# Down product of a streaming-encoder trunk: lower weight parts by ScalarE and an accumulating transfer, and one more seven-product pair

## The chip, the cores and the metric

The kernel runs on one core of one Trainium2 chip. The metric is device microseconds of one execution of the whole program. The kernel before takes 1934.27 us (median of 3 runs, 1934.19 to 1934.36).

A core has five engines with instruction streams of their own: TensorE (PE in the profile; its weight loads are PEld), VectorE (DVE), ScalarE (ACT), GpSimd (POOL) and SyncE (SP), which here only issues transfers. Each engine works through its instructions in order and waits on semaphores for the others. Transfers between HBM and the on-chip memory SBUF run on 16 DMA engines; matmuls accumulate in PSUM.

## The reference, cut to what matters

Two layers run over 256 tokens of width 2048. Layer 0 has a convolution mixer, layer 1 latent attention; each is followed by an MLP. The change lies in the MLP's second product alone:

```python
def sq_relu_mlp(h, w1, w2):
    return jnp.square(jax.nn.relu(h @ w1)) @ w2     # w1: 2048 x 8192, w2: 8192 x 2048

for layer in range(DEPTH):
    ...                                             # mixer, residual
    h = rms_norm(x, norm_mlp_g[layer])
    x = x + sq_relu_mlp(h, mlp_w1[layer], mlp_w2[layer])
```

All values are float32.

## The kernel before, in words

**Split products.** TensorE multiplies in a rounded 32-bit form (`fp32r`). To keep precision, each operand is split: the upper part `hi` is the value rounded by ScalarE (`AF.Copy` into an `fp32r` tile), the lower part `lo = raw - hi` comes from VectorE. A product is then three matmuls (`mm3`, lines 203 to 205): upper by upper, lower by upper, upper by lower. In the second of them the lower part is the activations', in the third it is the weights'. Only the third one reads the weights' `lo`.

**Weights.** `load` (line 153) brings a tile of 1 MB from HBM into one of three `raw` buffers, by SyncE's queue. `split` (line 181) splits it in two halves, `split_half` each: one ScalarE operation of 128x1024 (line 170) and one VectorE operation of 128x1024 (line 174). The `hi` and the `lo` tiles have six buffers each (`WB = 6`), which go round in the order in which the tiles are asked for: the seventh tile takes the buffer of the first, as soon as TensorE has read that for the last time.

**The MLP.** Each MLP is done in two halves of the 8192 hidden columns. A half is an up product (32 loads of `w1`, lines 655 and 656), which gives 32 blocks of 128 hidden rows, and a down product with those 32 blocks, added onto the residual `xs`. So there are four down products in a run: layer 0 halves 0 and 1, layer 1 halves 0 and 1.

**The down product.** It goes over the output columns in two column pairs of 2 x 512 (`n = 0` and `n = 2`). In each, the 32 hidden blocks are taken as 16 pairs of two blocks, and a pair with its 2 x 512 columns and the 2 x 128 tokens is a 2 x 2 by 2 x 2 block product. Two forms are used:

- A *plain quad* (`Sums.plain`, line 559) does the 8 block products, 24 matmuls of 128x512. Its weights are two row blocks, `j = 0` and `j = 1`, of 128x1024; TensorE does all of `j = 0` before `j = 1`.
- A *mixed quad* (`Sums.mixed`, line 546) does seven block products, 21 matmuls, of combined operands in the manner of Strassen and Winograd. VectorE forms the combined weights in `mixed_weights` (line 490: lines 505, 506 and 507 combine, line 498 makes the lower parts), and the combined activations in `mixed_inputs`. It takes four `hi` and four `lo` tiles where a plain quad takes two of each.

`MIXED` (line 44) lists the pairs done by seven products: eight of the 16 in the first three halves, seven in the last. The loop in `mlp` interleaves them with the plain quads by a rule of its own (`HEAD`, `TAIL`, the variable `upto`). With eight and eight, P for plain and M for mixed, the first column pair is P P M M P M M P M P M M P M P P and the second P M P M P M M P M P M P M M P P. In the last half only the first column pair uses this loop; the second goes through `product_A`, whose plain work comes in loads of four row blocks by 512 columns, with the mixed quads put between them.

**Results.** Some column blocks are added onto `xs` by transfers that GpSimd issues (line 578, `accum_op=ALU.add`), others by VectorE.

**Order.** Within the MLP the program's order on each engine is set by the framework's scheduler from the order in which the code is written; the rows that it gives for the changed places stand below.

Of the kernel before, what the change touches and what calls it, by code (L numbers as in the profile page):

```python
# [11 lines left out]
F32R = mybir.dt.float32r  # L12
BF16 = mybir.dt.bfloat16
I32 = mybir.dt.int32
AF = mybir.ActivationFunctionType
ALU = mybir.AluOpType
AX = mybir.AxisListType

P = 128
# [5 lines left out]
NB = 512  # L25
# [15 lines left out]
PAD_O = 56  # L41
WB = 6
LOOK = WB // 2 - 1
MIXED = {(layer, half): (0, 1, 4, 5, 8, 9, 12) + (13,) * (layer + half < 2) for layer in range(2) for half in range(2)}
N_MIXED = 4
HEAD, TAIL = (2, 1), 2

# [32 lines left out]
def trunk_kernel(  # L80
# [26 lines left out]
    nc = tc.nc  # L107
# [4 lines left out]
    wpool = ctx.enter_context(tc.tile_pool(name="wpool", bufs=2))  # L112
# [27 lines left out]
    def nm(s):  # L140
        uid[0] += 1
        return f"{s}_{uid[0]}"
# [10 lines left out]
    def load(srcs, nj, parts=1):  # L153

        raw = wpool.tile([P, nj, sum(src.shape[-1] for src in srcs)], F32, tag="raw", name=nm("raw"), bufs=3)
        for h in range(parts):
            js = slice(h * nj // parts, (h + 1) * nj // parts)
            at = 0
            for src in srcs:
                nc.sync.dma_start(raw[:, js, at : at + src.shape[-1]], src[:, js, :])  # L160
                at += src.shape[-1]
        return raw
# [14 lines left out]
    def split_half(raw, h, eng):  # L177

        return lower_half(*upper_half(raw, h), eng)

    def split(raw, eng):

        half = raw.shape[1] // 2
        parts = [split_half(raw, h, eng) for h in range(2)]

        def at_j(j):
            hi, lo = parts[j // half]
            return hi[:, j % half, :], lo[:, j % half, :]

        return at_j  # L190

# [3 lines left out]
    def rows(w, k0, nk, c0, n):  # L195

        return w[k0 * P : (k0 + nk) * P, c0 : c0 + n].rearrange(
            "(j p) n -> p j n", p=P
        )
# [331 lines left out]
    class Sums:  # L531
# [24 lines left out]
            for ps, i, (wh, wl) in work:  # L556
                mm3(ps, fh[:, i, :], fl[:, i, :], wh, wl, self.first(ps), end and any(ps is u for u in self.u))

        def plain(self, w, k, hi, lo, k0, end, middle=None):

            at_j = split(load([rows(w, k, 2, self.n * NB, 2 * NB)], 2), nc.vector)
            order = [(j, c, t) for j in range(2) for c in range(2) for t in range(T)]
            if end:
                order.sort(key=lambda r: r[1:])
            for i, (j, c, t) in enumerate(order):
                if middle is not None and 2 * i == len(order):
                    middle()
                wh, wl = (a[:, c * NB : (c + 1) * NB] for a in at_j(j))
                ps = self.e[t][c]
                mm3(ps, hi(k0 + j, t), lo(k0 + j, t), wh, wl, self.first(ps), end and j == 1)  # L570
# [38 lines left out]
    def mlp(layer, ssq, next_gain, finish=None, before=None, beside=None, after_up=None):  # L609

        with ExitStack() as cx:
# [22 lines left out]
            for hf in range(HALVES):  # L634
                last = hf == HALVES - 1
                ms = MIXED[layer, hf]
                mixed = sorted({p // 2 for p in ms})
                plain = [g for g in range(ng) if g not in mixed]
                gs = {}
                for g in range(ng):  # L640
# [4 lines left out]
                    for u in range(KC // 4):  # L645
# [3 lines left out]
                        for j in range(4):  # L649
                            k = 4 * u + j  # L650
# [12 lines left out]
                    if g in mixed or g in plain[len(plain) + len(mixed) - N_MIXED :]:  # L663
                        shape = [P, 2, 7, P] if g in mixed else [P, 4, S]
# [4 lines left out]
                    for b2 in range(2):  # L669
# [11 lines left out]
                        if g in mixed:  # L681
                            v = v.rearrange("p k (t n) -> p (k t) n", t=T)
                            h, l = gh[:, b2, : 2 * T, :], gl[:, b2, : 2 * T, :]
                        else:
                            h, l = (a[:, 2 * b2 : 2 * b2 + 2, :] for a in (gh, gl))
# [3 lines left out]
                w, k_lo = mlp_w2[layer], hf * nkh  # L689
# [9 lines left out]
                hi, lo = at_kt(0), at_kt(1)  # L699
# [8 lines left out]
                for n in range(0, NNB - 2 * split_end, 2):  # L708
                    sums = Sums(n, not last or split_end)
                    ks = [2 * p for p in ps]  # L710
                    at, head = 0, HEAD[n // 2]
                    for i, k in enumerate(ks):
                        upto = (len(ms) * (i - head + 1) + (head > 1) * (len(ks) - head - TAIL)) // (len(ks) - head - TAIL + 1)
                        while at < min(upto, len(ms)):
                            mixed_quad(sums, at)
                            at += 1
                        if i == len(ks) - TAIL + 1:
                            sums.join(room)
                        at_end = i == len(ks) - 1
                        sums.plain(  # L720
                            w, k_lo + k, hi, lo, k, at_end,
                            (lambda: [prepare(due.pop(0), out=room, rest=rest) for _ in range(len(due))]) if at_end else None,
                        )
                    sums.close(room)
                    while rest:
                        rest.pop(0)()
                    if last:
                        due += [n, n + 1]
# [29 lines left out]
    with ExitStack() as cx:  # L758
# [235 lines left out]
        with tc.manual_schedule():  # L994
# [214 lines left out]
            mean, scale = (tr_tile()[:, :S] for _ in range(2))  # L1209
# [58 lines left out]
            for m in range(NP):  # L1268
# [4 lines left out]
                for j in range(2):  # L1273
                    k = 2 * m + j
# [19 lines left out]
                for q in {NP - 3: (0, 1, 4), NP - 2: (5, 2, 3), NP - 1: (6, 7)}.get(m, ()):  # L1294
                    t, i = divmod(q, NNB)
# [74 lines left out]
    with ExitStack() as cx:  # L1370
# [58 lines left out]
        raws, parts = {}, {}  # L1429
# [270 lines left out]
        with tc.manual_schedule():  # L1700
# [23 lines left out]
            for k in range(KC):  # L1724
                u, j = divmod(k, 2)
# [23 lines left out]
            for k in range(KC):  # L1749
                u, j = divmod(k, 4)  # L1750
# [59 lines left out]
            for g in range(NG):  # L1810
                for i in range(HG):
                    h = g * HG + i
# [43 lines left out]
    with ExitStack():  # L1856
# [50 lines left out]
        def before(ssq):  # L1907

            for t in range(T):
# [4 lines left out]
                for n in range(NNB - 1):  # L1914
                    gained(t, n)

        mlp(1, ssq, None, finish, before, after_up=load_gf)


# [24 lines left out]
```

## Time and profile before

| | |
|---|---|
| median of the runs | 1934.27 us |
| profiled execution: span from first to last instruction | 1932.5 us |
| the four down products in that span | 478 to 641, 819 to 979, 1419 to 1582, 1760 to 1924 us |
| TensorE busy | 1921.0 us (99%) |
| VectorE busy | 1592.2 us (82%) |
| ScalarE busy | 1095.6 us (57%) |
| GpSimd busy | 249.0 us (13%) |
| moved from HBM | 363.68 MB |

The profile is of one execution. The median of the runs is 1.8 us above the span of that execution; what lies around the span is not in the profile. In a row that groups instructions, the number after x is the count, then come busy time in us, mean ns of one, and, after the second bar, the engine's idle time before these instructions with what ended it. In a row of the timeline the first number is the start in us from the span's start and the second the length; xN merges neighbours. In a row of transfers the last number is the median time from issue to landing.

### The profile page before, as it was taken

How to read it: one execution, taken by the hardware profiler on the slowest of the kernel's cores; microseconds unless marked ns; L12 is line 12 of the kernel's file. 1: busy time of each engine (PE TensorE's matmuls, PEld its weight loads, DVE VectorE, ACT ScalarE, POOL GpSimd, SP SyncE). 2: the span in 40 equal slices, each digit the busy share in tenths (PEclk: the TensorE clock that was granted, in tenths of full speed). 3: DMA queues.
4: the chain of work that ended last, by engine and by line, in shares of the span. 5: the costliest groups of instructions: out<-in, count | busy, mean ns of one | idle time of the engine just before them, and what ended most of it. 6: DMA issues, size and time to landing. Idle time of an engine off the chain costs nothing.

```text
span 1932.5 us, 28477 instructions
## 1 busy us (share of the span) xinstructions
PE 1921.0 (99%) x10725; PEld 1681.5 (87%) x10725; DVE 1592.2 (82%) x2457; ACT 1095.6 (57%) x1636; POOL 249.0 (13%) x208
## 2 busy tenths in 40 slices
PE   9999999999999999999999999999999999999998
PEld 8999888888888888888898998888888888888887
DVE  7999988877999776799976766877789987678998
ACT  5667755554555545555576655555555554455554
POOL 6999200000010100000001420000000010000000
PEclk9999999999999999999999999999999999999999
DMA  7766456665585866655656545465646776665774
GB/s 230 214 183 189 153 189 206 193 194 177 175 251 194 263 195 187 194 174 196 217 176 175 142 134 192 155 216 186 188 162 225 222 248 212 191 196 175 231 219 150
DMA packets 230427, 375.50 MB, mean 194 GB/s; under 512 B 16392, under 2 KB 107792, under 8 KB 230032
## 3 DMA queue, kind: packets, MB, share of 16 engines
q1 hardware_dynamic: 224640, 363.28, 58.7%
q0 software_dynamic: 4320, 7.87, 2.2%
q10 hardware_dynamic: 1328, 2.52, 0.4%
q8 instruction: 84, 1.38, 0.3%
q14 instruction: 55, 0.45, 0.1%
HBM read 363.68 MB, written 2.10 MB: 189 GB/s over the span
## 4 chain that ended last, share of the span: by engine, by line
PE 97%; DVE 2%; DMA 0%; ACT 0%; issue 0%; ACTq 0%; DVEq 0%
PE acc L655 24%; PE acc L205 15%; PE acc L203 15%; PE acc L204 15%; PE acc L656 13%; PE acc L823 8%; PE acc L1287 2%; DVE sum L910 1%; DMA xs<-in_x 0%; PE acc L1535 0%; PE acc L1566 0%; PE acc L1565 0%; PE acc L1536 0%; PE acc L1564 0%; PE acc L1537 0%; PE tr L267 0%
## 5 line engine op out<-in xcount | busy, mean ns | idle before, releaser
L174 DVE TENSOR_TENSOR lo<-raw,hi 128x1024 fp32r<-128x1024 f32 (+2 forms) x509 | 602.2, 1197 | 232.3 <-ACT hi L170 226.6
L170 ACT ACTIVATE hi<-raw 128x1024 fp32r<-128x1024 f32 (+2 forms) x574 | 583.9, 1036 | 361.1 <-PE acc L655 203.7
L655 PE MATMUL acc<-xt,hi 128*128 128x512 f32 x2048 | 710.6, 390 | 0.0
L656 PE MATMUL acc<-xt,lo 128*128 128x256 f32 x2048 | 577.5, 282 | 0.0
L655 PEld LDWEIGHTS acc<-xt,hi 128*128 128x128 f32 x2048 | 384.3, 188 | 80.7
L656 PEld LDWEIGHTS acc<-xt,lo 128*128 128x128 f32 x2048 | 387.1, 189 | 0.2
L497 ACT ACTIVATE hi<-raw 128x1024 fp32r<-128x1024 f32 x248 | 228.7, 948 | 228.3 <-DVE raw L505 134.0
L498 DVE TENSOR_TENSOR lo<-raw,hi 128x1024 fp32r<-128x1024 f32 x248 | 263.9, 1087 | 27.6 <-ACT hi L497 22.5
L203 PE MATMUL acc<-hi,sh 128*128 128x512 f32 x514 | 200.1, 389 | 0.0
L205 PE MATMUL acc<-lo,sh 128*128 128x512 f32 x514 | 200.1, 389 | 0.0
L203 PE MATMUL acc<-hi,gh 128*128 128x512 f32 (+1 forms) x516 | 200.0, 388 | 0.0
L205 PE MATMUL acc<-lo,gh 128*128 128x512 f32 (+1 forms) x516 | 199.9, 387 | 0.0
L204 PE MATMUL acc<-hi,gl 128*128 128x512 f32 (+1 forms) x516 | 199.9, 387 | 0.0
L823 PE MATMUL acc<-xt,hi 128*128 128x256 f32 x1024 | 180.2, 281 | 0.3 <-ACT b L1106 0.2
L204 PE MATMUL acc<-hi,sl 128*128 128x512 f32 x450 | 175.1, 389 | 0.0
L578 POOL DMA_DIRECT2D xs<-v x30 | 26.5, 994 | 1136.4 <-DVE lo L174 703.2
L910 DVE SCALAR_TENSOR_TENSOR sum<-ub,w_dw,sum 128x256 f32<-128x256 f32 x409 | 164.3, 481 | 3.6 <-ACT sum L880 3.0
L174 POOL TENSOR_TENSOR lo<-raw,hi 128x1024 fp32r<-128x1024 f32 x65 | 155.0, 2410 | 17.3 <-ACT hi L170 17.3
L823 PEld LDWEIGHTS acc<-xt,hi 128*128 128x128 f32 x1024 | 154.8, 188 | 1.1 <-ACT xt L1090 0.6
L823 PE MATMUL acc<-xt,lo 128*128 128x256 f32 x512 | 139.2, 279 | 0.0
L205 PEld LDWEIGHTS acc<-lo,sh 128*128 128x128 f32 x514 | 96.5, 188 | 20.4 <-DVE lo L498 0.3
L204 PEld LDWEIGHTS acc<-hi,gl 128*128 128x128 f32 x516 | 96.9, 188 | 19.9
(314 smaller groups left out, 2531.3 us busy)
## 6 DMA issues: line engine op xcount, KB each, us to landing
raw<-in_mlp_w SPq DMA_DIRECT2D x255, 1024.0 KB, 5.5
raw<-in_conv_w_pw SPq DMA_DIRECT2D x62, 512.0 KB, 5.1
raw<-in_conv_w_pw SPq DMA_DIRECT2D x16, 1024.0 KB, 5.1
raw<-in_mla_w_o SPq DMA_DIRECT2D x16, 1024.0 KB, 5.7
raw<-in_mla_w_kv_up SPq DMA_DIRECT2D x32, 256.0 KB, 3.9
xs<-v POOLq DMA_DIRECT2D x30, 256.0 KB, 7.8
raw<-in_mla_w_in SPq DMA_DIRECT2D x8, 576.0 KB, 3.8
raw<-in_mla_w_in SPq DMA_DIRECT2D x4, 1024.0 KB
```

What stands on the lines that cost most here:

```text
L170: nc.scalar.activation(hi, raw[:, js, :], AF.Copy)
L174: eng.tensor_tensor(lo, raw, hi.bitcast(F32), op=ALU.subtract)
L203: nc.tensor.matmul(ps, sh, mh, start=start, stop=False)
L204: nc.tensor.matmul(ps, sl, mh, start=False, stop=False)
L205: nc.tensor.matmul(ps, sh, ml, start=False, stop=stop)
L497: nc.scalar.activation(hi, src, AF.Copy)
L498: nc.vector.tensor_tensor(lo, src, hi.bitcast(F32), op=ALU.subtract)
L655: nc.tensor.matmul(ps[b], wh[:, bs], xhl(k), start=k == 0, stop=False)
L656: nc.tensor.matmul(ps[b][:, :S], wl[:, bs], xh(k), start=False, stop=k == KC - 1)
L823: nc.tensor.matmul(pss[c][b][:, :S], w[i][:, bs], (xh, xl)[j](k), start=k == i + j == 0, stop=end and k == k0 + nk - 1 and (i, j) == terms ...
L910: nc.vector.scalar_tensor_tensor(out=out, in0=ubs[c][:, w : w + S], scalar=tap(c, w), in1=base, op0=ALU.mult, op1=ALU.add)
L1287: nc.tensor.matmul(ps2[b][t], x_kt(k, t), w[:, bs], start=k == g == i == 0, stop=k == KC - 1 and i == len(group) - 1,)
```

## The change

Two edits.

1. `MIXED` gives the last half (layer 1, half 1) the eighth pair, 13, as in the other three.
2. `Sums.plain` gets a flag `by_sum`, set for the plain quads from number `head` up to the one before the last: five of the first column pair and six of the second. In such a quad the row block `j = 1` is split otherwise: ScalarE writes `lo = -raw`, rounded, and `hi`, and GpSimd issues a transfer that adds the same 512 KB of weights, read from HBM once more, onto `lo`. Row block `j = 0` is split as before. VectorE does one lower part of 128x1024 less in each, ScalarE one operation more. There are 11 such quads in each of the first three halves and five in the last, 38 in all.

```diff
-MIXED = {(layer, half): (0, 1, 4, 5, 8, 9, 12) + (13,) * (layer + half < 2) for layer in range(2) for half in range(2)}
+MIXED = {(layer, half): (0, 1, 4, 5, 8, 9, 12, 13) for layer in range(2) for half in range(2)}
...
+    def split_by_sum(src, raw, eng):
+
+        js = slice(raw.shape[1] // 2, raw.shape[1])
+        shape = [P, raw.shape[1] // 2, raw.shape[2]]
+        hi = wpool.tile(shape, F32R, tag="hi", name=nm("hi"), bufs=WB)
+        lo = wpool.tile(shape, F32R, tag="lo", name=nm("lo"), bufs=WB)
+        nc.scalar.activation(lo, raw[:, js, :], AF.Copy, scale=-1.0)
+        nc.gpsimd.dma_start(lo, src[:, js, :], accum_op=ALU.add)
+        nc.scalar.activation(hi, raw[:, js, :], AF.Copy)
+        parts = [split_half(raw, 0, eng), (hi, lo)]
+
+        def at_j(j):
+            h, l = parts[j // shape[1]]
+            return h[:, j % shape[1], :], l[:, j % shape[1], :]
+
+        return at_j
...
-        def plain(self, w, k, hi, lo, k0, end, middle=None):
+        def plain(self, w, k, hi, lo, k0, end, middle=None, by_sum=False):
 
-            at_j = split(load([rows(w, k, 2, self.n * NB, 2 * NB)], 2), nc.vector)
+            src = rows(w, k, 2, self.n * NB, 2 * NB)
+            raw = load([src], 2)
+            at_j = split_by_sum(src, raw, nc.vector) if by_sum else split(raw, nc.vector)
...
                             (lambda: [prepare(due.pop(0), out=room, rest=rest) for _ in range(len(due))]) if at_end else None,
+                            head <= i < len(ks) - 1,
```

How the order moves on ScalarE, in the first down product's first column pair, between two mixed quads (line 497 before, line 514 after). Before, a plain quad's two upper parts, `j = 0` and then `j = 1`:

```order
L170 ACTIVATE hi_5751<-raw_5749 128x1024
L170 ACTIVATE hi_5755<-raw_5749 128x1024
L497 ACTIVATE hi_5785<-raw_5783 128x1024
L497 ACTIVATE hi_5789<-raw_5783 128x512
L497 ACTIVATE hi_5796<-raw_5783 128x1024
L497 ACTIVATE hi_5800<-raw_5783 128x1024
L170 ACTIVATE hi_5827<-raw_5825 128x1024
L170 ACTIVATE hi_5831<-raw_5825 128x1024
```

After, for the same two quads:

```order
L200 ACTIVATE hi_5752<-raw_5750 128x1024
L198 ACTIVATE lo_5753<-raw_5750 128x1024
L170 ACTIVATE hi_5757<-raw_5750 128x1024
L514 ACTIVATE hi_5787<-raw_5785 128x1024
L514 ACTIVATE hi_5791<-raw_5785 128x512
L514 ACTIVATE hi_5798<-raw_5785 128x1024
L514 ACTIVATE hi_5802<-raw_5785 128x1024
L200 ACTIVATE hi_5829<-raw_5827 128x1024
L198 ACTIVATE lo_5830<-raw_5827 128x1024
L170 ACTIVATE hi_5834<-raw_5827 128x1024
```

The upper part of `j = 1` (line 200) now comes first, its negated copy (line 198) second, and the upper part of `j = 0` (line 170) third; the mixed quads' operations keep their places around them.

On GpSimd, at the end of the first column pair and the start of the second, after the change (line 199 is the new transfer, line 597 the old addition onto `xs`, line 578 before):

```order
L199 DMA lo_5634<-in_mlp_w 128x1024
L199 DMA lo_5753<-in_mlp_w 128x1024
L199 DMA lo_5830<-in_mlp_w 128x1024
L199 DMA lo_5949<-in_mlp_w 128x1024
L199 DMA lo_6026<-in_mlp_w 128x1024
L597 DMA xs<-v_6058 128x512
L597 DMA xs<-v_6060 128x512
L597 DMA xs<-v_6061 128x512
L597 DMA xs<-v_6059 128x512
L597 DMA xs<-v_6107 128x512
L597 DMA xs<-v_6110 128x512
L199 DMA lo_6200<-in_mlp_w 128x1024
```

Before, only the six additions onto `xs` stood here. Now five new transfers stand ahead of them and the next column pair's behind them, all in one queue.

## The prediction

> **What bounds the kernel now.** I read the page's first lines and the chain of waits first, then the groups of instructions kept apart by shape, then a table of the four down products.
>
> ```profile
> span 1932.5 us, 28477 instructions
> PE 1921.0 (99%) x10725; PEld 1681.5 (87%) x10725; DVE 1592.2 (82%) x2457; ACT 1095.6 (57%) x1636; POOL 249.0 (13%) x208
> ...
> PE 97%; DVE 2%; DMA 0%; ACT 0%; issue 0%; ACTq 0%; DVEq 0%
> ...
> L203 PE MATMUL acc<-hi,gh 128*128 128x512 f32 x508 | 197.7, 389 | 0.0
> L205 PE MATMUL acc<-lo,gh 128*128 128x512 f32 x508 | 197.7, 389 | 0.0
> L204 PE MATMUL acc<-hi,gl 128*128 128x512 f32 x508 | 197.7, 389 | 0.0
> L174 DVE TENSOR_TENSOR lo<-raw,hi 128x1024 fp32r<-128x1024 f32 x481 | 582.2, 1223 | 228.6 <-ACT hi L170 223.1 <-PE tr L267 2.6 <-PE acc L655 1.5
> L170 ACT ACTIVATE hi<-raw 128x1024 fp32r<-128x1024 f32 x546 | 566.1, 1055 | 357.6 <-PE acc L655 203.7 <-issue 54.7 <-PE acc L204 44.5
> ...
> core 0: us, PE busy (x) PEld busy (x) DVE busy (x) ACT busy (x) POOL busy (x), PEclk, DMA share, GB/s
> 478.00:641.00 163.00, 163.00 (x721) 135.00 (x720) 152.19 (x164) 92.70 (x104) 8.91 (x10) 1.00 0.65 209
> 819.00:979.00 160.00, 160.00 (x706) 132.21 (x705) 152.80 (x168) 90.15 (x106) 0.25 (x2) 1.00 0.57 191
> 1419.00:1582.00 163.00, 163.00 (x721) 134.99 (x720) 152.74 (x164) 92.88 (x105) 8.76 (x10) 1.00 0.65 209
> 1760.00:1924.00 164.00, 164.00 (x735) 136.16 (x734) 150.84 (x177) 91.30 (x115) 5.26 (x6) 1.00 0.62 199
> ```
>
> **TensorE sets the end.** It is 97% of the chain, and the last column of its groups, idle time before them, is 0.0. In the table each down product has its own count of matmuls by one pitch: 163.00 us for 721, or 0.226 us each (the 389 ns of a row is the pipelined length, not the pitch). VectorE is busy for 152 of the 163 us and so runs close behind, but TensorE never waits for it. Time taken from VectorE therefore buys nothing by itself; only fewer matmuls can, and any new wait of TensorE is paid in full.
>
> **What the matmuls give.** The eighth pair of seven products in the last half turns 24 matmuls into 21, for each of two column pairs: 6 x 0.226 = 1.4 us less. The order of the changed program agrees, with 6 rows of TensorE fewer. This is the whole possible gain.
>
> **What the new chain costs.** In 38 plain quads (11 in each of three halves, 5 in the last) the lower part of the second row block no longer comes from VectorE. ScalarE writes the upper part, then the negated upper part into `lo`, and only then a transfer of 512 KB adds the weights from HBM; TensorE may use `lo` once it has landed. So there is a clock to beat: from the moment ScalarE is through with its two operations to the third matmul of that row block. All that follows on TensorE is queued behind that matmul. I read both ends in the first down product, from three plain quads that the change touches (ScalarE's rows, then TensorE's):
>
> ```profile
> 494.70 1.99 ACT L170 ACTIVATE hi<-raw 128x1024 fp32r<-128x1024 f32 x2
> ...
> 501.64 0.39 PE L205 MATMUL acc<-lo,gh 128*128 128x512 f32 x1
> ...
> 510.49 1.99 ACT L170 ACTIVATE hi<-raw 128x1024 fp32r<-128x1024 f32 x2
> ...
> 516.60 0.39 PE L205 MATMUL acc<-lo,gh 128*128 128x512 f32 x1
> ...
> 518.41 0.39 PE L204 MATMUL acc<-hi,gl 128*128 128x512 f32 x1
> ...
> 518.86 0.39 PE L203 MATMUL acc<-hi,sh 128*128 128x512 f32 x1
> ...
> 519.52 1.99 ACT L170 ACTIVATE hi<-raw 128x1024 fp32r<-128x1024 f32 x2
> ...
> 526.80 0.39 PE L205 MATMUL acc<-lo,gh 128*128 128x512 f32 x1
> ```
>
> ScalarE's pair of operations stands at the same place of its order after the change (the order rows above), with another second operation of the same size. Behind **two** mixed quads it ends at 494.70 + 1.99 = 496.7 and at 512.5, and the matmul follows at 501.64 and 516.60: 4.9 and 4.1 us, mean **4.5 us**. Behind **one** mixed quad it ends at 521.5, and the matmul is at 526.80: 5.3 us. VectorE's relief may move this pair forward, but not far: the six `hi` buffers go round, so this row block takes the buffer of the plain quad before, whose last reader is the row at 518.41, over at 518.80. ScalarE then starts at 518.9 at the earliest and ends at 520.9: 5.9 us. I take the middle, **5.6 us**. With two mixed quads ScalarE waits for VectorE's chain inside the second of them, which begins only when the buffer of the plain quad before comes free, so relief does not help there.
>
> By the loop's own rule, 18 of the 38 stand behind two mixed quads (three per first column pair, two per second) and 20 behind one (two and four).
>
> **How long the transfer takes.** The trace has no transfer of this size that adds. The nearest are those that add 256 KB onto `xs`: five that were first in their queue while weight loads ran, then five in a stretch where the loads were nearly over, then the first product's two queues:
>
> ```profile
> xs<-v POOLq DMA_DIRECT2D x1, 256.0 KB, 5.7
> ...
> xs<-v POOLq DMA_DIRECT2D x1, 256.0 KB, 5.8
> ...
> xs<-v POOLq DMA_DIRECT2D x1, 256.0 KB, 7.0
> ...
> xs<-v POOLq DMA_DIRECT2D x1, 256.0 KB, 7.4
> ...
> xs<-v POOLq DMA_DIRECT2D x1, 256.0 KB, 7.8
> ...
> xs<-v POOLq DMA_DIRECT2D x5, 256.0 KB, 4.1
> ...
> q1 hardware_dynamic: 9012, 31.89, 57.8%
> q0 software_dynamic: 1125, 2.08, 6.9%
> ```
>
> In 163 us, 6.9% of the 16 engines is 11.2 us for 2.08 MB that add, 5.4 us per MB; the loads take 57.8%, 94.2 us for 31.89 MB, 3.0 us per MB. The 0.26 MB that a 512 KB transfer has more cost 0.26 x 5.4 = 1.4 us. Beside loads: mean of the five 6.7 + 1.4 = 8.1 us. Without them: 4.1 + 1.4 = 5.5 us. The loads hold the engines for 58% of the time, so 0.58 x 8.1 + 0.42 x 5.5 = **7.0 us**, my value. The bounds: 4.1 us, if the larger pieces cost no more than the small ones, and 7.8 + 1.4 = 9.2 us.
>
> The Trainium skill ("DMA: Bandwidth & Descriptors", section on the anatomy of a SWDGE DMA) fits 2.0 us plus bytes over 436 GB/s to a transfer issued from GpSimd; an estimate by it is 3.2 us for 512 KB, and by it no quad would wait. It gives 2.6 us for 256 KB, where the trace has 4.1 to 7.8 us, so the trace does not agree, and I go by the rows.
>
> **The sum of the waits.** Behind one mixed quad 7.0 - 5.6 = 1.4 us, times 20 is 28 us. Behind two 7.0 - 4.5 = 2.5 us, times 18 is 45 us. Together 73 us. The wait comes back at each quad, since each chain starts from a buffer that TensorE itself frees: a late TensorE makes the next chain late as well.
>
> **The rest of the edits.** ScalarE has one operation more per such quad, 38 x 1.06 = 40 us, inside products where it is busy for 93 of 163 us; the first row block's upper part is now third in its order, up to 1 us late behind two mixed quads, which lies inside the wait for the transfer as long as that is there. GpSimd has nothing else to do there; its six additions onto `xs` per column pair stand between two groups of the new transfers and don't touch them. The extra 20 MB from HBM take 38 x 0.52 MB x 5.4 = 107 us of each DMA engine; the loads are issued three tiles ahead, and I take nothing for them. The eighth pair burdens VectorE in the last column pair, where nothing is relieved:
>
> ```profile
> L498 DVE TENSOR_TENSOR lo<-raw,hi 128x1024 fp32r<-128x1024 f32 x186 | 225.5, 1221 | 27.6 <-ACT hi L497 22.5 <-PE acc L205 0.6
> L505 DVE TENSOR_TENSOR raw<-raw 128x1024 f32<-128x1024 f32 x62 | 75.5, 1218 | 0.2
> L507 DVE TENSOR_TENSOR raw<-raw 128x512 f32<-128x512 f32 x62 | 42.8, 691 | 1.7
> ...
> 1890.73 2.52 DVE L498 TENSOR_TENSOR lo<-raw,hi 128x1024 fp32r<-128x1024 f32 x2
> ...
> 1892.23 0.39 PE L205 MATMUL acc<-lo,sh 128*128 128x512 f32 x1
> ```
>
> A mixed quad costs VectorE 3 x 1.22 + 1.22 + 3 x 0.69 = 6.95 us against 21 x 0.226 = 4.75 us of TensorE. The pair moved costs it 6.95 instead of half a plain quad's 2 x 1.22 us, 5.7 us more, while TensorE has 4.75 - 2.7 = 2.0 us more ahead of the last mixed quad. VectorE falls back by 3.7 us there, and its lead is thin: the first of the two rows at 1890.73 is over about 0.3 us before TensorE uses it at 1892.23. Up to 3.4 us of waiting, nothing if a longer lead is carried in; I take 2 us.
>
> **Sum against the profiled execution:** 1932.5 - 1.4 + 73 + 2 = 2006 us of span. The median of the runs, 1934.27, lies 1.8 us above that span: **2008 us**, 3.8% slower.
>
> **The rivals.** *The transfer is hidden* (not slower): it lands within 4.1 us. For it speaks the row of five at 4.1 us, against it that this is half the size and has hardly any load beside it, and that the five lone ones beside loads took 5.7 us and more. Time: 1934.3 - 1.4 + 2 = 1935 us. It decides as soon as the transfer is under about 4.5 us. The fit of the Trainium skill above would give this time. *Only the short clock is missed*: 5.5 us, the transfer without loads. Then 18 x 1.0 = 18 us, and 1934.3 + 18 + 0.6 = 1953 us. For it: when TensorE waits, loads thin out. Against it: loads held 58% before the change. *The queues are the bound*: 9.2 us, since each quad of this kind adds 0.52 x 5.4 = 2.8 us of engine time to its own load. Then 20 x 3.6 + 18 x 4.7 = 157 us: 2092 us. For it, the 7.8 us row; against it, a longer quad leaves the engines more free time. *VectorE's relief pays*: over 0.2% faster needs 3.9 us where 1.4 us of matmuls go and the products have no idle time.
>
> **How the numbers follow.** About 0.2%, 3.9 us, is what a measurement of this kernel can tell from no change. Forecast (6.2 to 8.3 us per transfer): 0.57, by itself 1978 to 2057 us. Short clock only: 0.17. Queues: 0.12. Hidden: 0.12. Relief: 0.02. The first three are slower, 0.86; hidden is within 0.2%, 0.12; faster 0.02. For 8 in 10 the range takes in the short-clock case and reaches part of the way to the queues: 1940 to 2075 us.
>
> **What would show it.** In the changed profile the group of `lo` weight loads or matmuls waits for the transfer `lo<-in_mlp_w2`, some 38 times, 1 to 3 us each; the transfers' time to landing is near 7 us; VectorE's lower parts drop by 38; the down products grow from 163 to about 184 us, the up products stay. I am wrong if the landing is under 4.5 us, if TensorE's idle time in the down products stays near nothing, or if ScalarE reaches its two operations much earlier than these rows say.

## The result and the profile after

The changed kernel takes 2058.98 us (median of 4 runs, 2051.41 to 2062.82) against 1934.23 us before. The ratio is 1.0639, with a 95% interval of 1.0627 to 1.0652: 6.4% slower. The forecast was 2008 us, with a range of 1940 to 2075 us. The profiled execution has a span of 2061.0 us and is the longest of the four; against the span of before, 1932.5 us, it is 128.5 us longer, where the medians differ by 124.8 us.

The page of the changed kernel: the span, the chain by engine, the group of the third matmul of a block product, and two rows of transfers (the last number is the median from issue to landing).

```profile
span 2061.0 us, 28510 instructions
...
PE 82%; DMA 10%; DVE 4%; issue 3%; ACT 1%; ACTq 0%; DVEq 0%; POOLq 0%
...
L222 PE MATMUL acc<-lo,gh 128*128 128x512 f32 (+1 forms) x516 | 214.1, 420 | 80.6 <-DMA lo<-in_mlp_w 80.6
...
raw<-in_mlp_w SPq DMA_DIRECT2D x256, 1024.0 KB, 5.4
...
lo<-in_mlp_w POOLq DMA_DIRECT2D x38, 512.0 KB, 8.6
```

The chain was 97% TensorE and is 82% now; a tenth of it is the new transfer. The matmul that first reads `lo` (line 222 is the third matmul of `mm3`, line 205 before) waits for it, and the weight loads beside it have not become slower (5.4 us). The waits of TensorE, with their sum, their count and the longest, and then the four down products (the windows leave out the last 2 to 3 us of the third and the fourth):

```profile
PE acc L222 <- DMA lo<-in_mlp_w: 80.6, 24, 6.6
PE acc L220 <- ACT hi L514: 3.2, 6, 1.1
...
PE acc L222 <- DVE lo L174: 1.2, 1, 1.2
```

```profile
core 0: us, PE busy (x) PEld busy (x) DVE busy (x) ACT busy (x) POOL busy (x), PEclk, DMA share, GB/s
478.00:690.00 212.00, 186.65 (x786) 151.48 (x785) 148.31 (x158) 109.86 (x121) 20.26 (x23) 0.94 0.74 209
850.00:1060.00 210.00, 188.65 (x823) 154.09 (x822) 157.34 (x185) 114.18 (x145) 9.81 (x13) 0.95 0.64 186
1480.00:1690.00 210.00, 184.64 (x765) 149.49 (x764) 145.47 (x157) 107.95 (x119) 18.36 (x21) 0.93 0.71 198
1860.00:2050.00 190.00, 176.59 (x764) 142.25 (x763) 157.81 (x184) 102.99 (x127) 9.61 (x11) 0.98 0.64 191
```

24 of the 38 transfers are waited for, not all of them. And the column of the granted clock, 1.00 in each down product before, is 0.93 to 0.98. What that means shows at the first wait, in the timeline (start, length; in brackets the wait and what ended it):

```profile
501.51 0.39 PE L221 MATMUL acc<-hi,gl 128*128 128x512 f32 x1
505.82 0.79 PE L222 MATMUL acc<-lo,gh 128*128 128x512 f32 x1 [3.92 <-DMA lo<-in_mlp_w]
506.41 0.63 PE L220 MATMUL acc<-hi,gh 128*128 128x512 f32 x1
506.83 0.63 PE L221 MATMUL acc<-hi,gl 128*128 128x512 f32 x1
...
509.54 0.39 PE L222 MATMUL acc<-lo,gh 128*128 128x512 f32 x1
```

```profile
501.00:505.50 4.50, 0.90 (x4) 1.00 1.02 295
505.50:509.00 3.50, 3.18 (x8) 0.54 0.93 312
509.00:512.00 3.00, 3.00 (x14) 0.97 0.30 116
```

The second fence gives the same stretch in three windows: TensorE's busy time and matmuls, the granted clock, the share of the DMA engines, GB/s. The wait is followed by about 3.4 us at half clock: matmuls start every 0.43 us, and 8 stand in 3.5 us where 15 would fit. During the wait all 16 DMA engines are full; from issue to landing of each of the 38 transfers their share is 0.85 to 1.02.

Where the 128.5 us are, counted from the starts of the matmuls in the trace (a matmul's distance to the next one, less the usual one of its form):

| part | us |
|---|---|
| waits over 0.5 us at the 18 quads behind two mixed quads, 1.4 to 4.5 us each | 64.5 |
| waits over 0.5 us at 4 of the 20 quads behind one mixed quad | 19.1 |
| matmuls further apart in the 19 stretches of half clock | 34.6 |
| three waits in the last column pair, where there is no transfer | 2.9 |
| one wait in the attention after the second down product | 1.3 |
| six matmuls fewer | -1.4 |
| shorter delays and the rest | 7.5 |

### The profile page after: what moved, and what is told of

Its sections match the earlier page's. It is cut to its first block, busy times and chain, and to the rows that moved or that the text cites. A ratio compares the mean times of both kernels' runs of the same rounds, so it can differ in the third digit from the quotient of the medians.

```text
span 2061.0 us, 28510 instructions
## 1 busy us (share of the span) xinstructions
PE 1964.1 (95%) x10719; PEld 1701.9 (83%) x10719; DVE 1563.5 (76%) x2433; ACT 1140.5 (55%) x1678; POOL 282.0 (14%) x246
## 3 DMA queue, kind: packets, MB, share of 16 engines
q10 hardware_dynamic: 1328, 2.52, 0.4%
## 4 chain that ended last, share of the span: by engine, by line
PE 82%; DMA 10%; DVE 4%; issue 3%; ACT 1%; ACTq 0%; DVEq 0%; POOLq 0%
PE acc L674 22%; PE acc L675 12%; PE acc L222 12%; PE acc L220 11%; PE acc L221 11%; DMA lo<-in_mlp_w 10%; PE acc L843 8%; PE acc L1307 2%; DVE sum L930 1%; DVE lo L515 1%; ACT lo L198 0%; DVE raw L522 0%; DMA xs<-in_x 0%; PE acc L1555 0%; PE acc L1585 0%
## 5 line engine op out<-in xcount | busy, mean ns | idle before, releaser
L174 DVE TENSOR_TENSOR lo<-raw,hi 128x1024 fp32r<-128x1024 f32 (+1 forms) x465 | 554.3, 1201 | 346.7 <-ACT hi L170 341.5
L170 ACT ACTIVATE hi<-raw 128x1024 fp32r<-128x1024 f32 (+2 forms) x530 | 543.8, 1039 | 408.8 <-PE acc L674 212.9
L514 ACT ACTIVATE hi<-raw 128x1024 fp32r<-128x1024 f32 (+1 forms) x256 | 237.2, 950 | 248.0 <-DVE raw L522 114.5
L515 DVE TENSOR_TENSOR lo<-raw,hi 128x1024 fp32r<-128x1024 f32 (+1 forms) x256 | 273.0, 1088 | 44.1 <-ACT hi L514 39.9
L222 PE MATMUL acc<-lo,gh 128*128 128x512 f32 (+1 forms) x516 | 214.1, 420 | 80.6 <-DMA lo<-in_mlp_w 80.6
L199 POOL DMA_DIRECT2D lo<-in_mlp_w x38 | 34.4, 904 | 1456.2 <-ACT lo L198 1456.2
L220 PE MATMUL acc<-hi,gh 128*128 128x512 f32 (+1 forms) x516 | 211.3, 409 | 0.0
L221 PE MATMUL acc<-hi,gl 128*128 128x512 f32 (+1 forms) x516 | 210.9, 409 | 0.0
L222 PEld LDWEIGHTS acc<-lo,gh 128*128 128x128 f32 x516 | 104.1, 202 | 114.0 <-DMA lo<-in_mlp_w 90.8
L221 PEld LDWEIGHTS acc<-hi,gl 128*128 128x128 f32 x516 | 103.5, 201 | 22.5
```

Source lines behind the costliest of these rows:

```text
L170: nc.scalar.activation(hi, raw[:, js, :], AF.Copy)
L174: eng.tensor_tensor(lo, raw, hi.bitcast(F32), op=ALU.subtract)
L220: nc.tensor.matmul(ps, sh, mh, start=start, stop=False)
L221: nc.tensor.matmul(ps, sl, mh, start=False, stop=False)
L222: nc.tensor.matmul(ps, sh, ml, start=False, stop=stop)
L514: nc.scalar.activation(hi, src, AF.Copy)
```

## The experiments

Each edit is against the changed kernel. They leave out nothing of the computation. All of them, with the waits for a transfer and the length of all stretches of half clock in the down products, both of the profiled execution:

| kernel | us | ratio to before, 95% interval | waits for the transfer: us, times | half clock, us |
|---|---|---|---|---|
| the change | 2058.98 | 1.0639 [1.0627, 1.0652] | 80.6, 24 | 82 |
| pair alone | 1938.63 | 1.0022 [1.0012, 1.0031] | none | 0 |
| transfers alone | 2048.62 | 1.0595 [1.0578, 1.0611] | 72.0, 22 | 61 |
| behind one mixed quad | 1996.97 | 1.0327 [1.0310, 1.0343] | 43.3, 14 | 51 |
| behind two mixed quads | 2038.82 | 1.0536 [1.0522, 1.0550] | 64.4, 18 | 55 |
| VectorE's lower part | 1957.49 | 1.0122 [1.0107, 1.0137] | none | 3 |
| unread transfer | 1959.53 | 1.0132 [1.0117, 1.0147] | none | 0 |
| in order | 1947.43 | 1.0068 [1.0054, 1.0082] | none | 0 |
| 30 filling matmuls | 2078.76 | 1.0749 [1.0731, 1.0767] | 12.7, 6 | 7 |
| 16 filling matmuls | 2034.32 | 1.0517 [1.0502, 1.0531] | 22.2, 17 | 14 |
| not the first quad | 2037.37 | 1.0533 [1.0517, 1.0549] | 66.9, 24 | 58 |
| begun earlier | 2039.99 | 1.0543 [1.0527, 1.0559] | none | 38 |
| pair, GpSimd helps | 1940.28 | 1.0031 [1.0019, 1.0042] | none | 0 |

### Is it the transfer? VectorE's lower part, and an unread transfer

The first kernel leaves ScalarE's work and order as the change has them, but lets VectorE write the lower part:

```diff
-        nc.gpsimd.dma_start(lo, src[:, js, :], accum_op=ALU.add)
         nc.scalar.activation(hi, raw[:, js, :], AF.Copy)
+        lower_half(hi, lo, raw[:, js, :], eng)
```

> In the 38 quads VectorE writes the lower part of the second row block again, from ScalarE's upper part; there is no transfer onto it. ScalarE's negated copy, its place in ScalarE's order and the eighth pair stay. Theory (TensorE waits for the adding transfer, and all else follows from that): the 88 us of waits and the 35 us at half clock both go, 1935 to 1942 us. Rival (a good part comes from ScalarE's second operation and from the upper part of the first row block standing third in its order): 1960 us or more, and the matmuls then wait for ScalarE or VectorE.

The second adds to this a transfer of half the size that nobody waits for:

```diff
-        nc.gpsimd.dma_start(lo, src[:, js, :], accum_op=ALU.add)
+        nc.gpsimd.dma_start(scratch.rearrange("p (j n) -> p j n", j=1), src[:, js, :NB], accum_op=ALU.add)
```

> As the kernel with VectorE's lower part, but each of the 38 quads also starts an adding transfer of 256 KB (half the size of the change's) from the same weights into a tile that nobody reads. Theory (the wait for the data costs, the traffic does not): within 5 us of the kernel without the transfer, 1936 to 1946 us. Rival (the transfers hold up the weight loads on the 16 DMA engines): half the traffic leaves a good part of the loss, 1970 us or more, with matmuls or ScalarE waiting for loads of raw.

Measured: 1957.5 and 1959.5 us. Without the wait for the transfer 101 of the 125 us are gone. The traffic is not the main cause: with half of it still there, the time moves by 2 us, within the intervals. The whole traffic with nobody waiting was not run. The transfer's row in the page of the second kernel:

```profile
scratch<-in_mlp_w POOLq DMA_DIRECT2D x38, 256.0 KB, 5.7
```

The first expectation was missed all the same: 1935 to 1942 us was named and 1957.5 came, close to the rival's 1960. Some 19 us more than the pair alone takes (1938.6 us) remain with no transfer at all. The waits of TensorE in that kernel:

```profile
PE acc L222 <- DVE lo L174: 4.3, 5, 2.0
PE acc L220 <- ACT hi L170: 3.5, 11, 0.4
```

All but one are waits for the row block `j = 0`; the longest, 2.0 us, stands in the attention behind the second down product and has 3.4 us of half clock behind it. The rows of ScalarE and VectorE in the first plain quad between mixed ones show why (lines 199, 198 and 170: upper part of `j = 1`, its negated copy, upper part of `j = 0`):

```profile
495.95 1.05 ACT L199 ACTIVATE hi<-raw 128x1024 fp32r<-128x1024 f32 x1
496.90 1.04 ACT L198 ACTIVATE lo<-raw 128x1024 fp32r<-128x1024 f32 x1
497.84 1.05 ACT L170 ACTIVATE hi<-raw 128x1024 fp32r<-128x1024 f32 x1
...
497.97 2.36 DVE L174 TENSOR_TENSOR lo<-raw,hi 128x1024 fp32r<-128x1024 f32 x2 [0.67 <-ACT lo L198]
```

`j = 0`, which TensorE wants first, is served last on both engines. So a third kernel has the same operations in the other order:

```diff
+        first = split_half(raw, 0, eng)
         hi = wpool.tile(shape, F32R, tag="hi", name=nm("hi"), bufs=WB)
...
-        parts = [split_half(raw, 0, eng), (hi, lo)]
+        parts = [first, (hi, lo)]
```

> As the kernel with VectorE's lower part and no transfer, which took 1957.5 us, but the first row block is split first, then ScalarE's negated copy and the second row block. Theory (the 19 us above the pair alone come from the order, by which VectorE and ScalarE serve the second row block ahead of the first that TensorE needs sooner): 1939 to 1942 us. Rival (they come from ScalarE's third operation, 38 x 1.0 us, which makes the next mixed quads late): 1950 us or more.

Measured: 1947.4 us, between the two. VectorE starts the lower part of `j = 0` 1.9 us earlier than the second of the two above, counted from the start of the down product (at 495.86 - 477.9 = 18.0 against 497.97 + 1.2 - 479.3 = 19.9 us), and the waits of the plain quads for `j = 0` are gone. Of the 19 us, 10 were the order. The other 9 stay. What is left of the edit is ScalarE's additional operation, and the waits now stand at the mixed quads, 6.7 us where the pair alone has 3.1, and 1.7 us in the attention:

```profile
PE acc L221 <- ACT hi L515: 3.6, 7, 1.1
PE acc L223 <- DVE lo L516: 3.1, 7, 0.7
```

(Lines 515 and 516 are the upper and lower parts of mixed quads there.) VectorE also has to let ScalarE's copy finish before it writes the same `lo`, and is idle for 0.48 us on it at the first of these quads; what each of the two costs was not separated.

### Does the half clock cost, or only show?

In the 18 quads behind two mixed quads, matmuls with zeros are put ahead of the one that waits; they add zero to the sums.

```diff
+                if by_sum and fill and (j, c, t) == (1, 0, 0):
+                    nc.tensor.matmul(ps, hi(k0 + j, t), wh, start=self.first(ps), stop=False)
+                    nc.tensor.matmul(ps, lo(k0 + j, t), wh, start=False, stop=False)
+                    for _ in range(fill):
+                        nc.tensor.matmul(ps[:, :P], zeros, ident, start=False, stop=False)
+                    nc.tensor.matmul(ps, hi(k0 + j, t), wl, start=False, stop=False)
+                    continue
```

> The whole change; in the 18 plain quads behind two mixed quads, 30 matmuls of 128x128 with zeros (by an estimate 0.11 us each, 3.3 us, from the half-clock-free pitch of 0.226 us for 512 columns and the shortest matmuls of the trace) stand ahead of the matmul that waits for the transfer. They add zero to the sums. Theory (after a wait of about 3 us TensorE runs a stretch of 3.4 us at half clock, which is a cost beside the wait): the filling lies inside the wait and the half clock behind these quads goes, 18 x 1.7 = 30 us less, about 2029 us. Rival (the half clock only shows in the records, or is a consequence of something else, and costs nothing by itself): 2055 to 2075 us.

> As the first filling, which had 30 zero matmuls that ran as 60 of 0.112 us, 6.7 us, longer than the wait: now 16, which makes 32 x 0.112 = 3.6 us, about the wait behind two mixed quads after the change. Theory (the half clock is a cost of its own, 1.7 us per wait): the waits stay covered by the same time and the half clock behind these 18 quads goes: 2059 - 18 x 1.7 = 2028 us, and nearly all windows of 0.50 clock are gone but those after the first quads of the second column pairs. Rival (TensorE loses nothing by the half clock, because the quad after the wait is bound by something else): 2059 us again.

The first try took 2078.8 us, 20 us more than the change, above even the rival's range. It decides nothing: each of the 30 ran as two instructions, and 6.9 us of filling per quad (123.4 / 18) is longer than the wait that it filled. With 16 the filling fits, and the time falls to 2034.3 us, 24.7 us less than the change, though TensorE is kept from its work for as long as before. The groups of the two kernels, 30 first, then 16, and with 16 the first and the last down product (columns as above):

```profile
L596 PE MATMUL acc<-ident,scratch 128*128 128x128 f32 x1080 | 123.4, 275 | 0.0
```

```profile
L596 PE MATMUL acc<-ident,scratch 128*128 128x128 f32 x576 | 67.2, 275 | 0.0
```

```profile
478.00:680.00 202.00, 194.47 (x931) 162.38 (x930) 147.55 (x158) 108.52 (x121) 20.29 (x23) 0.98 0.76 214
...
1830.00:2000.00 170.00, 164.72 (x785) 136.51 (x784) 140.50 (x155) 93.56 (x107) 9.66 (x11) 1.00 0.68 199
```

576 instructions in 67.2 us take the place of 62 us of waits (those over 0.5 us fall from 87.7 to 25.8 us), and the clock is back near 1.00; the two stretches of half clock that are left stand behind first quads of second column pairs, which are not filled. So the half clock is a cost beside the wait: 24.7 us net, 1.4 us for each of the 18, and about 30 us if the 5 us of filling beyond the waits are added. The theory had 1.7 us for each.

Which waits bring it can be read from all the kernels together. In each trace the stretches of half clock begin on a grid of 3.413 us that runs on through the whole execution. Between the kernel's first 13 and last 8 us there are 92 such stretches, and in the window of this grid ahead of each TensorE is idle for 49% of the time or more; no window with more than 54% is followed by full clock. So the place in the grid counts beside the length. By an estimate from these shares a single idle time under 1.7 us cannot bring the half clock, one over 3.7 us always does, and two short ones in the same window can.

### Which quads wait? One kind at a time

```diff
-                            head <= i < len(ks) - 1,
+                            head <= i < len(ks) - 1 and ahead == 1,
```

(`ahead` is the number of mixed quads that stand right before the plain quad.)

> The change at the 20 plain quads behind one mixed quad alone; those behind two are split by VectorE. My prediction had 28 us of waits for these 20. The trace after the change has waits at only 4 of them, 19 us, at the first quad of a column pair behind the six additions onto xs. Theory (from the trace): 1934 + 19 + 4 x 1.7 to 3.4 of half clock, less 1.4: 1958 to 1966 us, nearly all of it in three or four places of 5 to 7 us. Rival (they wait little after the change only because the longer quads behind two mixed ones gave the loads and buffers time): 1.4 us each and the half clock, 1975 us or more.

And the same with `ahead == 2`:

> The change at the 18 plain quads behind two mixed quads alone. Theory (from the trace after the change): waits of 64 us and 18 x 1.7 = 31 us of half clock, less 1.4 and plus 3 for the last column pair: 2030 to 2035 us. By the prediction's own terms, 45 us and no half clock: 1980 us. Rival (the waits behind two mixed quads rest on the quads behind one, which hold the queue): under 2000 us.

TensorE's waits with the 20 quads behind one, then with the 18 behind two:

```profile
PE acc L222 <- DMA lo<-in_mlp_w: 43.3, 14, 5.3
```

```profile
PE acc L222 <- DMA lo<-in_mlp_w: 64.4, 18, 4.4
```

Behind two mixed quads, each of the 18 waits, 3.6 us on average; 2038.8 us, a little above what was expected, and far above the 1980 us by the prediction's terms. Behind one, the expectation from the trace was wrong: 1997.0 us, not 1958 to 1966, and the rival (1975 us or more) holds. Alone, 14 of these 20 wait 3.1 us on average, where with the whole change only 4 wait longer than 0.5 us. The two kinds alone cost 62.6 and 104.4 us, each with the eighth pair in it; both together cost 125: a wait at one quad spares the next. In the trace of the whole change, the second wait, ScalarE's rows, and in the last row the matmul that first reads the next plain quad's `lo`:

```profile
522.25 0.39 PE L221 MATMUL acc<-hi,gl 128*128 128x512 f32 x1
...
524.37 1.04 ACT L200 ACTIVATE hi<-raw 128x1024 fp32r<-128x1024 f32 x1
525.31 1.04 ACT L198 ACTIVATE lo<-raw 128x1024 fp32r<-128x1024 f32 x1
...
526.02 0.60 PE L222 MATMUL acc<-lo,gh 128*128 128x512 f32 x1 [3.37 <-DMA lo<-in_mlp_w]
...
537.95 0.39 PE L222 MATMUL acc<-lo,gh 128*128 128x512 f32 x1
```

While TensorE waits (522.25 to 526.02 us), ScalarE already makes the next plain quad's upper part and negated copy, without an idle time of its own: the buffers that it writes were free. So the next transfer starts at about the time at which TensorE goes on, and TensorE first has its delayed matmuls, partly at half clock, a mixed quad and the next quad's first row block to do. It comes to the new `lo` at 537.95 us, 11.6 us after the copy ended. Over the whole changed kernel the time from the end of that copy to the moment at which TensorE would start the matmul is 11.0 us on average behind one mixed quad, where the prediction took 5.6, and 5.5 us behind two, where it took 4.5. With the quads behind one alone it is 5.3 to 7.8 us at the 14 that wait. That the head start is the cause is read from these rows and from the two kernels' numbers; no run varied it by itself.

### The first quad of the second column pair

```diff
-                            head <= i < len(ks) - 1,
+                            head + (n > 0) <= i < len(ks) - 1,
```

> The whole change but for the first of the plain quads in the second column pair of three halves, whose transfer stands in GpSimd's queue behind the six additions onto xs; there VectorE writes the lower part. Theory (the queue of the additions makes that wait, 6.6, 5.0 and 6.7 us, and each brings half a clock for 3 to 7 us): 2059 - 18 - 3 x 2.5 = 2033 us, and the other waits stay. Rival (the time is only passed on: as seen where one kind of quad alone was changed, the next quad behind then waits instead): 2045 us or more.

Measured: 2037.4 us, 21.6 us less than the change, nearer to the theory (2033) than to the rival (2045 or more). Part of the time is passed on: the next touched quad of the pair, which did not wait before, now waits 2.0, 3.8 and 1.3 us. But the reason given holds for two of the three places only. The rows of the change in the first half (GpSimd issues the last two additions onto `xs`, then the transfer; TensorE's row before and after the wait), then those in the second half, and the transfers issued in 25 us around the first place:

```profile
581.15 1.75 POOL L597 DMA_DIRECT2D xs<-v  x2 [8.73 <-ACT hi L200]
582.43 1.39 POOL L199 DMA_DIRECT2D lo<-in_mlp_w  x1
...
589.84 0.39 PE L221 MATMUL acc<-hi,gl 128*128 128x512 f32 x1
596.70 0.79 PE L222 MATMUL acc<-lo,gh 128*128 128x512 f32 x1 [6.47 <-DMA lo<-in_mlp_w]
...
963.65 0.86 POOL L199 DMA_DIRECT2D lo<-in_mlp_w  x1 [27.20 <-ACT lo L198]
...
972.67 0.79 PE L222 MATMUL acc<-lo,gh 128*128 128x512 f32 x1 [4.80 <-DMA lo<-in_mlp_w]
```

```profile
raw<-in_mlp_w SPq DMA_DIRECT2D x3, 1024.0 KB, 10.9
lo<-in_mlp_w POOLq DMA_DIRECT2D x2, 512.0 KB, 11.7
xs<-v POOLq DMA_DIRECT2D x2, 256.0 KB, 10.1
```

In the first half it is 596.7 - 582.4 = 14.3 us from issue to the end of TensorE's wait: two additions are ahead in the queue, and the weight loads of the same time need 10.9 us themselves. The third half is alike, with a transfer of 14.4 us. In the second half GpSimd issues no additions at all, the transfer takes 9.0 us as others do, and TensorE waits all the same, since it is ready for the matmul 4.5 us after ScalarE's copy, not 8.4 us as in the other two. So the additions account for about 5 us of each transfer behind them, and the wait in the second half is a late chain.

### Begun earlier

The load, the negated copy and the transfer of a touched quad are put ahead of the last mixed quad before it, and the quad's first row block is split ahead of the second one's upper part:

```diff
+                            if at == min(upto, len(ms)) - 1 and head <= i < len(ks) - 1:
+                                begun = begin_sum(rows(w, k_lo + k, 2, n * NB, 2 * NB))
                             mixed_quad(sums, at)
```

> The whole change, but the load, the negated copy and the adding transfer of each of the 38 quads begin ahead of the last mixed quad before it, one quad (4.7 us) earlier in the order of ScalarE and of the queues. Theory (the transfer is only too late, not too costly): with 4.7 us more than before, waits of 1.4 to 4.5 us mostly vanish and the half clock with them, 1933 to 1945 us; the 6.6 us at the first quads of the second column pairs may leave 2 us each. Rival (the lo buffers go round, so that the chain cannot start earlier than its buffer comes free; or the loads become late): 1980 us or more.

Measured: 2040.0 us; the rival holds, in its second form: loads are late. No matmul waits for the transfer any more, although it takes 9.5 us now. Now the mixed quads wait. The chain, the group of the first matmuls of mixed quads, the transfer, and what ScalarE waits for (line 521: the upper parts of mixed quads):

```profile
PE 72%; DMA 11%; DVE 10%; ACT 4%; issue 3%; ACTq 0%; SPq 0%; DVEq 0%
...
L227 PE MATMUL acc<-hi,sh 128*128 128x512 f32 x512 | 213.6, 417 | 58.2 <-ACT hi L521 57.9
...
lo<-in_mlp_w POOLq DMA_DIRECT2D x38, 512.0 KB, 9.5
```

```profile
ACT hi L521 <- DVE raw L529: 120.7, 56, 3.2
ACT hi L521 <- DMA raw<-in_mlp_w: 97.5, 34, 6.2
```

With the change, ScalarE waited 3 times, 11.0 us, for a mixed quad's load; now 34 times. The plain quad's tile is loaded ahead of the mixed quad's, which TensorE needs first, and holds one of three `raw` buffers for longer. The wait was moved, not removed. That the longer hold of the `raw` buffer is the reason is read from the order; a fourth buffer was not tried.

### The pair alone, the transfers alone

```diff
-                            head <= i < len(ks) - 1,
+                            False,
```

> The eighth pair of seven products alone; all plain quads are split by VectorE as before. My step said 1.4 us of matmuls less and 2 us of waits more: 1935 us, within 0.2% of before. By the trace after the change (waits of 0.96, 1.30 and 0.60 us in the last column pair): 1934.2 - 1.4 + 2.9 = 1935.8 us. Rival (those waits came from the delayed chain, not from the pair): 1932.9 us. Another (VectorE, with nothing to relieve it, falls back in the whole last product): 1940 us or more.

The other kernel takes the list `MIXED` of before:

> The transfers alone, seven pairs of seven products in the last half as before. Theory (the loss is the transfers', the pair is nearly nothing): 2055 to 2060 us. Rival (a part of the loss is the pair's): below 2050 us.

The pair alone takes 1938.6 us, 0.22% (0.12 to 0.31%) more than before and about 3 us more than expected. Its waits, all in the last column pair:

```profile
PE acc L220 <- ACT hi L514: 1.9, 5, 0.7
...
PE acc L222 <- DVE lo L515: 1.2, 2, 0.7
```

The transfers alone take 2048.6 us, 10.4 us less than both edits: a part of the loss is the pair's, as the rival had it. Part of the difference is the pair itself; the other part is that the eighth pair changes the row of quads in the first column pair of the last half: with seven, one of its touched quads stands behind two mixed ones, with eight, three do. Accordingly the plain quads of that half have two waits for a transfer, 3.9 and 1.2 us, without the pair, and three, 4.2, 2.8 and 3.2 us, with it.

To see whether the pair pays once VectorE is relieved where it is late, GpSimd takes one of two lower parts in three of the plain loads there:

```diff
-                wjs.append(load_split([rows(w, k_lo + ks[0], len(ks), n * NB, NB)], len(ks)))
+                relief = nc.gpsimd if banks is not None and n == blocks[0] and u < nu - 1 else None
+                wjs.append(split(load([rows(w, k_lo + ks[0], len(ks), n * NB, NB)], len(ks)), nc.vector, relief))
```

> The eighth pair alone, and in the first column block of the last column pair GpSimd writes one of the two lower parts of each plain load but the last, in 2.4 us by its rows at the start of the trace, where VectorE takes 1.2. Theory (the pair alone is slower since VectorE falls back by 3.7 us there): with VectorE relieved by 1.2 us for each, the waits of 3 us go and 1.4 us of matmuls are saved: 1933 us, within 0.2% of before. Rival (GpSimd's 2.4 us make the plain loads late, or the waits come from ScalarE and the buffers): 1937 us or more.

Measured: 1940.3 us, no better than the pair alone; the rival holds. One of the three places in this kernel, GpSimd's and VectorE's rows:

```profile
1862.15 2.67 POOL L174 TENSOR_TENSOR lo<-raw,hi 128x1024 fp32r<-128x1024 f32 x1 [12.14 <-ACT hi L170]
...
1863.05 3.46 DVE L516 TENSOR_TENSOR lo<-raw,hi 128x1024 fp32r<-128x1024 f32 x2 [0.49 <-ACT hi L515]
```

Two such operations of VectorE take 2.52 us elsewhere; beside GpSimd's they take 3.46. Most of the 1.2 us of relief is given back at once. None of the kernels run beats the one before.

## Why the prediction was right, and where it was not

The sign, the cause and the place were right: TensorE sets the end, the wait for the transfer comes on top in full, the down products grow (the first from 163 to 201 us) and the up products stay (178 us each). 2059 us lies in the range, but just above the likeliest case's own range (1978 to 2057), and the terms of the sum differ:

- **The transfer: 7.0 us, measured 8.6.** The 256 KB that the larger transfer has more cost 2.9 us (8.6 against 5.7 for the unread one, in another kernel), not 1.4. And the mean with 42% of a case without loads was wrong: while these transfers run the engines are full (share 0.85 to 1.02, the transfers included), and the average of 58% comes from other moments.
- **The rivals.** 8.6 us lies between the forecast's longest transfer (8.3) and that of the rival in which the queues are the bound (9.2 us); nothing of the hidden transfer (4.1) or of the short one (5.5) shows, the shortest of the 38 takes 6.7 us. VectorE's relief bought nothing, as said.
- **Behind two mixed quads: 45 us, measured 64.** All 18 wait, as predicted, but 3.6 us each instead of 2.5. The transfer adds 1.6 us, and the 0.4 us from the end of ScalarE's copy to the issue, which the sum left out, add to it; the distance from ScalarE's pair to the matmul takes 1.0 us off, since it was 5.5 us and not 4.5.
- **Behind one: 28 us over 20 quads, measured 19 at four.** The step that failed is "the wait comes back at each quad, since each chain starts from a buffer that TensorE itself frees". The buffer is free before the wait, so a wait gives the next chain a head start: the distance that the sum took as 5.6 us is 11.0 us on average. That ScalarE reaches its two operations much earlier was one of the prediction's own signs of being wrong, and it came true here. Alone, these quads cost more than predicted (62.6 us), beside the others less.
- **The additions onto `xs` "don't touch" the transfers: they do, in two places.** Two of the four waits behind one mixed quad, 13.4 us and the half clock after them, stand behind additions, where the transfer takes 14.2 and 14.4 us. There are not six additions in each column pair, as the prediction says: the second half has none, and its wait of 5.0 us at the same place comes from a chain that is late. Without these three quads the time is 21.6 us shorter.
- **The half clock was not in the sum: about 25 to 35 us.** The filled kernel shows 24.7 us net for 18 waits; the matmuls' distances in the change add up to 34.6 us for all. This is the largest term that was missing. The rule could have been had beforehand: the Trainium skill ("TensorE: Matmul & The Clock Gate", Part 1, the HAM clock gate) says that after an idle window of about 3.4 us the clock falls to half, and that it needs a busy window of that length to recover. The trace agrees on the half and on the length: in the change a stretch of half clock follows each of the 19 waits of 3.2 us and more and none of those of 2.8 us and less; 15 of the stretches last 3.41 us, three 6.83 and one 10.24 us, multiples of the same window. It does not take a whole idle window, though. In the other kernels some waits between 2.7 and 3.5 us brought one and some did not, and in the kernel begun earlier some waits of about 2 us did: a window of the grid that is about half idle is enough.
- **ScalarE's operation "lies inside the wait": so it does, but only as long as the wait is there.** Without the wait, the operation and its order cost 19 us.
- **The eighth pair: -1.4 + 2 = +0.6 us, measured +4.2.** Three mixed quads now stand in a row twice in the last column pair, and there the waits are. That VectorE falls back by more than was reckoned is argued from this; the one try to relieve it gave no gain.

With 8.6 us in the prediction's own sum, 20 x 3.0 + 18 x 4.1 + 0.6 = 134 us would have given 2069 us. That is close to 2059 by luck: it has 41 us too much behind one mixed quad, 9 too much behind two, and nothing for the half clock.

## What to carry to other kernels

A wait on the engine that sets the end costs more than its own length where it brings the clock down; price a TensorE wait of about 3 us or more at roughly 1.4 times its length, as here (64 us of waits, 25 us of half clock), and expect it of two shorter waits too when they stand within 3.4 us. Work moved from an engine that is not the bound to a transfer trades a short duration (1.2 us) for a latency (8.6 us), and is worth looking at only where the consumer is that far away; find that distance in the trace first, and take the transfer's time from moments with the same load on the DMA engines. And a chain of waits is not a sum: measure each kind alone and together before dividing the loss among them.

## What the runs showed of the hardware that was not expected

- After a wait of about 3 us TensorE ran 3.41 us at half clock, matmuls every 0.43 us in place of 0.226; zero matmuls in the wait prevented it and won 24.7 us. The stretches begin on a fixed grid of 3.413 us, each behind a window of it that was idle for 49% or more.
- An adding transfer of 256 KB took 5.7 us beside the weight loads, one of 512 KB 8.6 us, and 14.3 us behind two additions in the same queue, while the 1 MB weight loads of the whole run stayed at 5.4 us in the median (5.5 before). A packet of 4 KB that adds held its DMA engine for 328 ns in the median, one of a load for 159 ns.
- VectorE's lower parts, 1.26 us each in a pair, took 1.73 us beside one on GpSimd (2.52 and 3.46 us for two). The Trainium skill ("SBUF — State Buffer", section "Who interferes with whom") says that an operation of VectorE with two inputs in SBUF contends with one of GpSimd that reads SBUF; these rows agree.
- A matmul of 128x128 with both operands in full 32-bit form ran as two instructions of 0.112 us.
